# A fused two-layer decoder step on one core: gates and a gelu computed through the tanh, and two margins in the order of emission

## The chip, the core and the metric

The kernel runs on one core of a Trainium2 chip. The time is device time in microseconds (us) of one execution of the whole program; lower is better.

## What is computed

Two layers are run for 256 prompt rows and 32 sample rows (8 sequences of 4) together, width 1024, in fp32. One layer is

```
x = x + 1/2 * SwiGLU_1(rmsnorm(x))
h = rmsnorm(x); u, v, q, k, v_att, q_idx, k_idx, w_idx, gate_A, gate_B = split(h @ w_in)
a = gelu(u) * (W_s (causal, per channel group) @ rmsnorm(gelu(v)) + b_s)
attn = attention of q over the best min(256, L/4) keys, chosen by an index score (8 heads, 2 key heads)
m = sigmoid(gate_A) * (a @ w_pa) + sigmoid(gate_B) * (attn @ w_pb);  x = x + m @ w_out
x = x + 1/2 * SwiGLU_2(rmsnorm(x))
```

The sample rows attend over 2048 cached positions as well, which lie in pages: keys, values and index keys come through a page table. The gelu is the tanh form, gelu(u) = u/2 * (1 + tanh(sqrt(2/pi) * (u + 0.044715 u^3))).

## The kernel before, in words

All activations lie transposed, features on the 128 partitions and the 288 rows in the free dimension. The weight matrices are cut into **units** of up to 8 blocks of 128x128. A unit's weights land in a `raw` tile, ScalarE copies them to fp32r as `wh`, VectorE makes the remainder `wl` (`unit_split`, L487), and TensorE runs three matmuls a block, `wh` and `wl` against high and low parts of the activations (`unit_mm`, L510), 24 a unit, into one of three accumulators `mm`. An evacuation (`ev_...`, L730 to L856) then takes the accumulator. The mixer's units come in the order k_idx with w_idx, q_idx, q, k, v, v_att, seven of gate_B, u, then gate_A and w_pa in turn, the last gate_B, w_pb and w_out (L863 to L877). The units of w_pb carry `need=(l, "attn")` (L875): none is emitted before the attention is complete.

Everything else of the mixer runs between the units as generators: norms, index scores and the search of the threshold (31 rounds, `sample`, L1201), prompt heads (`two_heads`, L1101, and `head_values`, L1149), spatial gating (`spatial_group`, L1050), scores and attention over cached pages (`sample_qk`, L1166, `attend`, L1397). Their matmuls go to five side banks `s`. Cached pages come as 1 MB tiles through a ring of four (`loader`, L681), issued on SyncE (SP), 8 DMAs a tile of keys or values; a slot is free again after its matmuls (`drop_tile`).

**The order is made while the program is emitted.** There is one instruction stream per engine, and the class `Clocks` (L112) estimates for every emitted instruction when it would run; `Engine.cost` (L223) prices it and adds 1283 ns on ScalarE when `TABLES` (L218) says that the function table changes. After every block of a unit, `hook` (L448) lets each generator go one step on. A generator yields until its conditions hold on these clocks:

```
def ready(*aps, on="PE", slack=0.0):
    slack -= PRM["margin"] if on == "PE" else 0          # margin = 300 ns
    while clocks.after(aps, by=on) > max(clk["PE"], clk[on]) + slack:
        yield
```

`use_tile` (L660) calls `ready` on a ring tile, so its matmuls are emitted once the clocks have it landed 300 ns ago. `palloc` (L365) hands out a side bank whose last readers end, on the clocks, at most 50 ns after TensorE's clock. `go` (L404) yields at most six times before an instruction on ScalarE or VectorE whose input isn't ready. What the clocks say is only an order: at run time each engine waits on semaphores.

An evacuation of u is Gelu on ScalarE into `ta`, a multiplication with the spatial result `sv` on VectorE, and `Pair.put` (L591): a copy to fp32r on ScalarE and the remainder on VectorE. Gates are a Sigmoid on ScalarE and later a multiplication on VectorE. In the profile all instructions carry L294, the line of the helper that emits them, so groups are told apart by tile names: `mm` accumulators, `s` side banks, `ring` cached pages, `b` 288-wide blocks, `lg`/`lgs` scores, `wh`/`wl`/`raw` weights.

Of the kernel before, what the change touches and what calls it, by code (L numbers as in the profile page):

```python
# [9 lines left out]
F32 = mybir.dt.float32  # L10
# [3 lines left out]
AF = mybir.ActivationFunctionType  # L14
OP = mybir.AluOpType
# [4 lines left out]

PRM = dict(norm=(1, 4000.0), pi=(2, 4000.0), qk=(1, 5000.0), head=(1, 2000.0), sp=(0, 5000.0), at=(0, 4000.0),
           sam=(0, 1e9), turn=2000.0, turn_n=6, early=7, ahead=4000.0, warm=10, pool=300.0, psplit=0, raw=2,
           resc=2, margin=300.0, order='qi q k v va')
L = 2
D = 1024
KT = 8
# [3 lines left out]
T = SEQ + DB * DT  # L30
# [11 lines left out]
LW = 2052  # L42
NB = 67
RING = 4

O_ID, O_SW, O_SEL = 0, 128, 256
O_CM, O_WSM, O_WSS, O_WM, O_MN, O_HM, O_ER = 384, 768, 896, 928, 992, 1056, 1064
# [167 lines left out]


class Engine:
    TABLES = {AF.Exp: "exp", AF.Silu: "silu", AF.Gelu_apprx_tanh: "gelu", AF.Sigmoid: "sigmoid"}  # L218

    def __init__(self, clocks, name, engine):  # L220
        self.c, self.n, self.e, self.table, self.mode = clocks, name, engine, None, None
# [1 line left out]
    def cost(self, k, a, kw):  # L223
# [33 lines left out]
        if self.n == "S":  # L257
            psum = str(getattr(a[1], "space", "")).endswith("PSUM")
            w = (51 if psum else 93) + 0.833 * n + 93 * ("accum_out" in kw)
            w += 94 * (hasattr(kw.get("scale"), "ap") + hasattr(kw.get("bias"), "ap"))  # L260
            t = self.TABLES.get(a[2])
            if t and t != self.table:
# [42 lines left out]
def trunk(ctx, tc, A, OUT):  # L305
    nc = tc.nc
    V, S, P, Q, PE = nc.vector, nc.scalar, nc.gpsimd, nc.sync, nc.tensor
    clocks = Clocks()
    clk = clocks.t
    V, S, P, Q, PE = (Engine(clocks, n, e) for n, e in (("V", V), ("S", S), ("P", P), ("Q", Q), ("PE", PE)))  # L310
# [4 lines left out]
    hlp = ctx.enter_context(tc.tile_pool(name="hlp", bufs=3))  # L315
    rgp = ctx.enter_context(tc.tile_pool(name="rgp", bufs=RING))
    tp = ctx.enter_context(tc.tile_pool(name="tp", bufs=2))
# [21 lines left out]
    x = cp.tile([128, KT, T], F32, name="x")  # L339
# [23 lines left out]
    bank_last = {}  # L363

    def palloc(dt=F32):  # L365
        while True:
            for tag in free_banks:
                if tag not in bank_last or clocks.after((), [bank_last[tag]]) <= clk["PE"] + 50:
                    free_banks.remove(tag)
                    t = bank_last[tag] = pss.tile([128, 512], dt, tag=tag, name=tag)  # L370
                    return t, tag
            yield
# [18 lines left out]
    def spawn_front(g):  # L391
        gens.insert(0, ((-1, 1e9), g))
# [5 lines left out]
    def ready(*aps, on="PE", slack=0.0):  # L398

        slack -= PRM["margin"] if on == "PE" else 0  # L400
        while clocks.after(aps, by=on) > max(clk["PE"], clk[on]) + slack:
            yield

    def go(eng, *aps):  # L404

        for _ in range(PRM["turn_n"]):
            if hurry[0] or clocks.after(aps, by=eng) <= max(clk["PE"], clk[eng]) and clk[eng] <= clk["PE"] + PRM["turn"]:
                return
            yield
# [124 lines left out]
    def sumsq(n, src):  # L534
        while squares[0] != n:
            yield
        if n == 0:
            S.activation(acc[:, :T], src, AF.Square)
        else:
            q = tp.tile([128, T], F32, tag="sq", name="sq")  # L540
            S.activation(q, src, AF.Square)
            yield from go("V", q)
            V.tensor_tensor(acc[:, :T], acc[:, :T], q, op=OP.add)
        squares[0] = (n + 1) % KT
# [13 lines left out]
    def rms_gen(key, full=True):  # L558
        yield from ready(acc)
        ps, tag = yield from palloc()  # L560
        sums(ps, acc)
        rs = mp.tile([128, 3], F32, tag="rs", name="rs", bufs=2)
        ms = mp.tile([128, 3], F32, tag="ms", name="ms", bufs=2)
        V.tensor_scalar(ms, ps[:, :3], 1.0 / D, EPS, op0=OP.mult, op1=OP.add)
        pfree(tag)
        P.tensor_tensor(rs, ms, mhalf.to_broadcast([128, 3]), op=OP.pow)
        yield from ready(rs)
        ps, tag = yield from palloc()
        c0 = 0 if full else 256
        spread(ps, lambda j: rs[:, j:j + 1], full)  # L570
        rb = mp.tile([128, T], F32, tag="rb", name="rb", bufs=2)
        copy(rb[:, c0:], ps[:, c0:T])
        pfree(tag)
        rstd_now[key] = (rb, rs)

    class Pair:
# [11 lines left out]
            V.scalar_tensor_tensor(lo.t, t, g, h.t.bitcast(F32), op0=OP.mult, op1=OP.subtract)  # L588
            self.h[n], self.l[n] = h, lo

        def put(self, n, t):  # L591
            h, lo = Block(F32R), Block(F32R)
            yield from go("S", t)
            S.activation(h.t, t, AF.Copy)
            yield from go("V", h.t)
            V.tensor_tensor(lo.t, t, h.t.bitcast(F32), op=OP.subtract)
            self.h[n], self.l[n] = h, lo

        def __call__(self, k):
# [56 lines left out]
    tiles = {}  # L656
# [3 lines left out]
    def use_tile(key):  # L660
        while key not in tiles:
            yield
        yield from ready(tiles[key])
        return tiles[key]

    def drop_tile(key):
# [14 lines left out]
    def loader():  # L681
        yield from wait("idx")
        n = 0
        for key in want:
# [4 lines left out]
            else:  # L689
                while n - state["used"] >= RING:  # L690
                    yield
# [21 lines left out]
    def mixer(l, xp, key, nxt, next_gain, next_rms):  # L713
        M = {"q": [], "sq": [], "qi": [], "vg": {}, "sv": {}, "ma": {}, "sb": {}}
        xs, a_, t_, m_ = Pair(), Pair(), Pair(), Pair()
# [88 lines left out]
        def ev_u(n):  # L804
            def ev(ps):
                t = tp.tile([128, T], F32, tag="ta", name="ta")
                S.activation(t, ps[:, :T], AF.Gelu_apprx_tanh)
                yield from go("V", t)
                V.tensor_tensor(t, t, M["sv"][n].t, op=OP.mult)
                M["sv"][n].free()  # L810
                yield from a_.put(n, t)
            return ev

        def ev_ga(n):
            def ev(ps):
                t = M["sa", n] = tp.tile([128, T], F32, tag="ta", name="ta")
                S.activation(t, ps[:, :T], AF.Sigmoid)
                yield
            return ev

        def ev_pa(n):
            def ev(ps):
                b = Block()
                M["ma"][n] = b
                V.tensor_tensor(b.t, ps[:, :T], M.pop(("sa", n)), op=OP.mult)
                yield
            return ev

        def ev_gb(n):
            def ev(ps):  # L830
                b = Block()
                M["sb"][n] = b
                S.activation(b.t, ps[:, :T], AF.Sigmoid)
                yield
            return ev

        def ev_pb(n):
            def ev(ps):
                t = tp.tile([128, T], F32, tag="ta", name="ta")
                V.tensor_tensor(t, ps[:, :T], M["sb"][n].t, op=OP.mult)  # L840
                m = tp.tile([128, T], F32, tag="tb", name="tb")
                V.tensor_tensor(m, t, M["ma"][n].t, op=OP.add)
                M["sb"][n].free()
                M["ma"][n].free()
                yield from m_.put(n, m)
            return ev

        def ev_out(n):
            def ev(ps):
                V.tensor_tensor(x[:, n], ps[:, :T], x[:, n], op=OP.add)  # L850
                yield from nxt.add(n, next_gain(n))
                yield from sumsq(n, x[:, n])
                if n == KT - 1:
                    spawn_front(rms_gen(next_rms))
            return ev
# [6 lines left out]
        for nm in PRM["order"].split() + ["gb", "u"]:  # L862
            n, ev = evs_[nm]  # L863
# [671 lines left out]
    def square(n):  # L1535
        q = tp.tile([128, T], F32, tag="sq" if n > 3 else "tb", name="sq")
        if n > 3:
            S.activation(q, x[:, n], AF.Square)
        else:
            P.tensor_tensor(q, x[:, n], x[:, n], op=OP.mult)  # L1540
        return q
# [9 lines left out]
    for n in range(KT):  # L1551
# [3 lines left out]
        if 0 < n < 4:  # L1555
            q = square(n)
# [3 lines left out]
    for n in range(4, KT):  # L1560
        q = square(n)
# [27 lines left out]
    def idle(what):  # L1589
        n = 0  # L1590
        while not what():
            hurry[0] = True
            if n > 4:
                clk["PE"] += 200
            hook()
            evacs(True)
            n += 1
            assert n < 1000
        hurry[0] = False
        return n  # L1600
# [8 lines left out]
    for i, u in enumerate(units):  # L1609
# [3 lines left out]
        n = idle(lambda: u["need"] is None or u["need"] in flags)  # L1613
# [84 lines left out]
```

## Time and profile before

| | |
|---|---|
| median of 3 runs | 1549.53 us (1547.25 to 1549.8) |
| the profiled execution, its own time | 1547.6 us |
| its span, first to last instruction | 1545.8 us |
| busy: TensorE / its weight loads | 1515.0 / 1444.6 us |
| busy: VectorE / ScalarE / GpSimd | 976.0 / 768.6 / 52.5 us |
| mean granted TensorE clock | 0.998 |

The two mixers run from about 228 to 572 us and from about 996 to 1337 us; the rest is the four SwiGLU blocks. PE is TensorE, PEld its weight loads, DVE VectorE, ACT ScalarE, POOL GpSimd, SP SyncE, a trailing q the engine's sequencer. A matmul's end is modelled, so "busy" says that TensorE had work, not that it ran at its peak. A wait is idle time of an engine that ended with a semaphore; a wait for several is put down to the one that came last.

### The profile page before, as it was taken

How to read it: one execution, taken by the hardware profiler on the slowest of the kernel's cores; microseconds unless marked ns; L12 is line 12 of the kernel's file. 1: busy time of each engine (PE TensorE's matmuls, PEld its weight loads, DVE VectorE, ACT ScalarE, POOL GpSimd, SP SyncE). 2: the span in 40 equal slices, each digit the busy share in tenths (PEclk: the TensorE clock that was granted, in tenths of full speed). 3: DMA queues.
4: the chain of work that ended last, by engine and by line, in shares of the span. 5: the costliest groups of instructions: out<-in, count | busy, mean ns of one | idle time of the engine just before them, and what ended most of it. 6: DMA issues, size and time to landing. Idle time of an engine off the chain costs nothing.

```text
span 1545.8 us, 32344 instructions
## 1 busy us (share of the span) xinstructions
PE 1515.0 (98%) x12110; PEld 1444.6 (93%) x12110; DVE 976.0 (63%) x1987; ACT 768.6 (50%) x1241; POOL 52.5 (3%) x65
## 2 busy tenths in 40 slices
PE   8999999999999999999999999999999999999999
PEld 7999998987879999999999999989887799999999
DVE  6666558875554666665556665588855547666643
ACT  5444444657773454444444444446578634544432
POOL 1000011100000000000000000201000000000000
PEclk9999999999999999999999999999999999999999
DMA  7666555587887665545545555556888854454563
GB/s 256 213 206 192 174 156 161 179 268 239 261 273 232 209 191 194 166 165 164 168 158 167 171 159 162 155 165 191 272 250 276 278 176 164 162 166 164 162 181 112
DMA packets 162558, 299.75 MB, mean 194 GB/s; under 512 B 21857, under 2 KB 108386, under 8 KB 162402
## 3 DMA queue, kind: packets, MB, share of 16 engines
q10 hardware_dynamic: 61552, 212.95, 43.0%
q1 hardware_dynamic: 100850, 84.73, 18.0%
q8 instruction: 97, 1.59, 0.4%
q14 instruction: 59, 0.48, 0.1%
HBM read 294.83 MB, written 2.77 MB: 193 GB/s over the span
## 4 chain that ended last, share of the span: by engine, by line
PE 77%; issue 14%; DMA 4%; ACT 2%; DVE 2%; SPq 1%; POOL 1%; POOLq 0%; DVEq 0%; ACTq 0%
PE mm L294 71%; PE s L294 6%; DMA raw<-in_win 1%; DMA ring<-in_kT 1%; DMA ring<-in_cv 1%; SPq L294 1%; ACT L294 1%; POOL rs L294 0%; DVE b L294 0%; DVE wl L294 0%; ACT b L294 0%; ACT wh L294 0%; DMA b<-in_ws 0%; DMA x<-in_x 0%; ACT lg L294 0%
## 5 line engine op out<-in xcount | busy, mean ns | idle before, releaser
L294 PE MATMUL mm<-b,wh 128*128 128x288 f32 x6560 | 1327.5, 298 | 4.8 <-DVE b L294 2.6
L294 PEld LDWEIGHTS mm<-b,wh 128*128 128x128 f32 x6560 | 1047.5, 188 | 24.4 <-issue 14.3
L294 PE MATMUL mm<-b,wl 128*128 128x288 f32 x3280 | 965.9, 294 | 2.3 <-DVE wl L294 1.6
L294 ACT ACTIVATE wh<-raw 128x1024 fp32r<-128x1024 f32 (+3 forms) x421 | 435.0, 1034 | 548.9 <-PE mm L294 538.9
L294 DVE TENSOR_TENSOR wl<-raw,wh 128x1024 fp32r<-128x1024 f32 (+3 forms) x421 | 503.2, 1197 | 264.4 <-ACT wh L294 259.7
L294 PEld LDWEIGHTS mm<-b,wl 128*128 128x128 f32 x3280 | 615.9, 188 | 3.5 <-DVE wl L294 3.5
L294 DVE TENSOR_TENSOR ta<-mm,rb 128x288 f32<-128x288 f32 x88 | 40.3, 458 | 55.6 <-PE mm L294 49.3
L294 ACT ACT_TABLE_LOAD x54 | 69.3, 1283 | 9.5 <-DMA ring<-in_cv 3.7
L294 DVE TENSOR_TENSOR tc<-mm,tb 128x288 f32<-128x288 f32 x88 | 40.3, 458 | 52.6 <-PE mm L294 52.2
L294 POOL TENSOR_TENSOR rs<-ms,mhalf 128x3 f32<-128x3 f32 x8 | 11.4, 1423 | 1111.2 <-DVE ms L294 1035.4
L294 DVE TENSOR_SCALAR_CACHE_REDUCE jk<-z,ci 128x513 bf16<-128x513 f32 x62 | 46.6, 751 | 2.2
L294 DVE TENSOR_TENSOR tb<-ta,rb 128x288 f32<-128x288 f32 x88 | 39.7, 452 | 4.9 <-ACT ta L294 4.9
L294 DVE TENSOR_TENSOR b<-tc,b 128x288 fp32r<-128x288 f32 x88 | 39.7, 451 | 0.0
L294 PE MATMUL s<-ring,qz 128*32 128x256 f32 x512 | 34.2, 383 | 4.4 <-DMA ring<-in_kT 4.4
L294 ACT ACTIVATE b<-tc 128x288 fp32r<-128x288 f32 x88 | 37.7, 429 | 1.5 <-DVE tc L294 1.0
L294 ACT ACTIVATE ta<-ta 128x288 f32<-128x288 f32 x88 | 37.8, 430 | 0.8 <-DVE ta L294 0.7
L294 ACT ACTIVATE jk<-z,ci 128x513 bf16<-128x513 f32 x30 | 21.8, 726 | 30.0 <-DVE ci L294 28.5
L294 PE MATMUL s<-ring,b 128*32 128x256 f32 x512 | 33.9, 382 | 2.5 <-DMA ring<-in_cv 2.5
L294 DVE SCALAR_TENSOR_TENSOR x<-mm,x 128x288 f32<-128x288 f32 x32 | 14.7, 458 | 31.4 <-PE mm L294 31.4
L294 PEld LDWEIGHTS s<-ring,qz 128*32 128x32 f32 x512 | 16.4, 109 | 16.5 <-issue 5.8
L294 PEld LDWEIGHTS s<-ring,b 128*32 128x32 f32 x512 | 16.7, 109 | 15.2 <-DMA ring<-in_cv 5.3
L294 ACT ACTIVATE b<-s 128x16 fp32r<-128x16 f32 (+2 forms) x62 | 16.4, 280 | 26.3 <-PE s L294 13.1
(193 smaller groups left out, 845.3 us busy)
## 6 DMA issues: line engine op xcount, KB each, us to landing
raw<-in_wup ACTq DMA_DIRECT2D x173, 512.0 KB, 3.5
raw<-in_win ACTq DMA_DIRECT2D x96, 512.0 KB, 4.3
ring<-in_kT SPq DMA_DIRECT2D x256, 128.0 KB, 3.3
ring<-in_cv SPq DMA_DIRECT2D x256, 128.0 KB, 4.0
raw<-in_wdn ACTq DMA_DIRECT2D x64, 448.0 KB, 3.3
raw<-in_wdn ACTq DMA_DIRECT2D x32, 512.0 KB, 3.5
raw<-in_wpa ACTq DMA_DIRECT2D x16, 512.0 KB, 4.2
raw<-in_wpb ACTq DMA_DIRECT2D x16, 512.0 KB, 3.7
```

What stands on the lines that cost most here:

```text
L294: r = f(*a, **kw)
```

## The change

Sigmoid goes out: the gates keep tanh(x/2), and as sigmoid(x) = (1 + tanh(x/2))/2, the later multiplication becomes (tanh + 1) * product, and the half that both gates then lack is applied in `ev_out`. The gelu of u is spelled out: Square on ScalarE, the cubic's bracket and two multiplications on VectorE, Tanh on ScalarE, (tanh + 1) times u * sv on VectorE, and the half rides in the scale of `put`. gelu(v) stays as it is. `TABLES` forgets Sigmoid and has no entry for Tanh, so the clocks charge no table for it. A ring tile is used when the clocks have it landed 1800 ns ago instead of 300; a side bank is taken when its last readers ended 250 ns ago instead of in at most 50.

```
-           resc=2, margin=300.0, order='qi q k v va')
+           resc=2, margin=300.0, late=1500.0, order='qi q k v va')
+GELU = float(np.sqrt(2.0 / np.pi))
-    TABLES = {AF.Exp: "exp", AF.Silu: "silu", AF.Gelu_apprx_tanh: "gelu", AF.Sigmoid: "sigmoid"}
+    TABLES = {AF.Exp: "exp", AF.Silu: "silu", AF.Gelu_apprx_tanh: "gelu"}
     def palloc(dt=F32):
-                if tag not in bank_last or clocks.after((), [bank_last[tag]]) <= clk["PE"] + 50:
+                if tag not in bank_last or clocks.after((), [bank_last[tag]]) <= clk["PE"] - 250:
-        def put(self, n, t):
+        def put(self, n, t, half=None):
...
-            S.activation(h.t, t, AF.Copy)
+            kw = {} if half is None else dict(scale=half)
+            S.activation(h.t, t, AF.Copy, **kw)
             yield from go("V", h.t)
-            V.tensor_tensor(lo.t, t, h.t.bitcast(F32), op=OP.subtract)
+            if half is None:
+                V.tensor_tensor(lo.t, t, h.t.bitcast(F32), op=OP.subtract)
+            else:
+                V.scalar_tensor_tensor(lo.t, t, half, h.t.bitcast(F32), op0=OP.mult, op1=OP.subtract)
     def use_tile(key):
-        yield from ready(tiles[key])
+        yield from ready(tiles[key], slack=-PRM["late"])
         def ev_u(n):
                 t = tp.tile([128, T], F32, tag="ta", name="ta")
-                S.activation(t, ps[:, :T], AF.Gelu_apprx_tanh)
+                y = M["sv"][n]
+                S.activation(t, ps[:, :T], AF.Square)
+                V.tensor_tensor(y.t, ps[:, :T], y.t, op=OP.mult)
                 yield from go("V", t)
-                V.tensor_tensor(t, t, M["sv"][n].t, op=OP.mult)
-                M["sv"][n].free()
-                yield from a_.put(n, t)
+                V.tensor_scalar(t, t, GELU * 0.044715, GELU, op0=OP.mult, op1=OP.add)
+                V.tensor_tensor(t, t, ps[:, :T], op=OP.mult)
+                yield from go("S", t)
+                S.activation(t, t, AF.Tanh)
+                yield from go("V", t)
+                V.scalar_tensor_tensor(t, t, 1.0, y.t, op0=OP.add, op1=OP.mult)
+                y.free()
+                yield from a_.put(n, t, 0.5)
         def ev_ga(n):
-                S.activation(t, ps[:, :T], AF.Sigmoid)
+                S.activation(t, ps[:, :T], AF.Tanh, scale=0.5)
         def ev_pa(n):
-                V.tensor_tensor(b.t, ps[:, :T], M.pop(("sa", n)), op=OP.mult)
+                V.scalar_tensor_tensor(b.t, M.pop(("sa", n)), 1.0, ps[:, :T], op0=OP.add, op1=OP.mult)
         def ev_gb(n):
-                S.activation(b.t, ps[:, :T], AF.Sigmoid)
+                S.activation(b.t, ps[:, :T], AF.Tanh, scale=0.5)
         def ev_pb(n):
-                V.tensor_tensor(t, ps[:, :T], M["sb"][n].t, op=OP.mult)
+                V.scalar_tensor_tensor(t, M["sb"][n].t, 1.0, ps[:, :T], op0=OP.add, op1=OP.mult)
         def ev_out(n):
-                V.tensor_tensor(x[:, n], ps[:, :T], x[:, n], op=OP.add)
+                V.scalar_tensor_tensor(x[:, n], ps[:, :T], 0.5, x[:, n], op0=OP.mult, op1=OP.add)
```

## Rows read from the trace of the kernel before

**Rows 1.** The page, busy time, share of the span and instructions of each engine.
```profile
PE 1515.0 (98%) x12110; PEld 1444.6 (93%) x12110; DVE 976.0 (63%) x1987; ACT 768.6 (50%) x1241; POOL 52.5 (3%) x65
```
**Rows 2.** Busy by stretch: length, PE, PEld, DVE, ACT, POOL, clock, DMA, GB/s.
```profile
228.00:302.00 74.00, 74.00 (x672) 63.20 (x672) 64.16 (x210) 38.51 (x73) 11.42 (x7) 1.00 0.49 156
302.00:360.00 58.00, 55.43 (x506) 49.64 (x505) 45.36 (x158) 31.12 (x67) 4.68 (x10) 1.00 0.81 252
360.00:460.00 100.00, 91.27 (x810) 77.94 (x808) 54.33 (x161) 77.30 (x141) 2.46 (x7) 0.98 0.84 263
...
1071.00:1127.00 56.00, 54.76 (x505) 49.42 (x505) 45.38 (x157) 31.14 (x66) 4.69 (x10) 1.00 0.86 265
1127.00:1226.00 99.00, 92.23 (x822) 78.55 (x822) 54.70 (x161) 78.51 (x145) 2.47 (x7) 1.00 0.85 269
```
**Rows 3.** Waits of TensorE, whole run: total us, times, longest us.
```profile
PE s L294 <- DMA ring<-in_kT: 4.4, 4, 2.4
PE s L294 <- DVE b L294: 4.3, 2, 2.6
...
PE s L294 <- DMA ring<-in_cv: 2.5, 3, 1.7
PE s L294 <- POOL b L294: 2.3, 3, 0.8
```
**Rows 4.** Timeline near 445 us on ACT, DVE and PE: start us, us, what.
```profile
445.12 1.28 ACT L294 ACT_TABLE_LOAD   x1 [0.90 <-DVE b L294]
...
446.72 1.05 ACT L294 ACTIVATE wh<-raw 128x1024 fp32r<-128x1024 f32 x1
...
448.37 0.42 DVE L294 TENSOR_TENSOR b<-s,b 128x256 fp32r<-128x256 f32 x1 [1.83 <-ACT b L294]
...
448.86 0.90 PE L294 MATMUL s<-cst,lg 128*128 128x128 f32 x3 [2.60 <-DVE b L294]
```
**Rows 5.** Busy by stretch around that wait.
```profile
448.30:451.70 3.40, 2.85 (x11) 2.67 (x12) 3.29 (x9) 1.98 (x7) 0.00 (x0) 0.50 0.81 242
444.90:448.30 3.40, 1.35 (x12) 1.12 (x10) 1.65 (x3) 3.17 (x5) 0.00 (x0) 1.00 0.94 324
```
**Rows 6.** Timeline of PE, the two longest waits for ring tiles.
```profile
329.30 1.02 PE L294 MATMUL s<-ring,qz 128*32 128x256 f32 x10 [2.38 <-DMA ring<-in_kT]
...
407.65 1.05 PE L294 MATMUL s<-ring,b 128*32 128x256 f32 x10 [1.74 <-DMA ring<-in_cv]
```
**Rows 7.** Groups of ACT: count, busy us, mean ns, idle before; whole run, then 360:462.
```profile
L294 ACT ACT_TABLE_LOAD x54 | 69.3, 1283 | 9.5 <-DMA ring<-in_cv 3.7 <-DVE wl L294 2.3 <-DVE b L294 1.8
...
L294 ACT ACT_TABLE_LOAD x24 | 30.8, 1283 | 2.2 <-DVE wl L294 1.0 <-DVE b L294 0.9
```
**Rows 8.** Timeline of ACT at the first gelu of v.
```profile
302.32 1.28 ACT L294 ACT_TABLE_LOAD   x1
303.61 0.41 ACT L294 ACTIVATE b<-mm 128x288 f32<-128x288 f32 x1
```
**Rows 9.** Groups by shape, whole run: count, busy us, mean ns, idle before.
```profile
L294 ACT ACTIVATE ta<-ta 128x288 f32<-128x288 f32 x88 | 37.8, 430 | 0.8 <-DVE ta L294 0.7
...
L294 DVE SCALAR_TENSOR_TENSOR x<-mm,x 128x288 f32<-128x288 f32 x32 | 14.7, 458 | 31.4 <-PE mm L294 31.4
...
L294 DVE TENSOR_TENSOR x<-mm,x 128x288 f32<-128x288 f32 x16 | 7.3, 458 | 4.7 <-PE mm L294 4.7
...
L294 DVE TENSOR_TENSOR ta<-ta,b 128x288 f32<-128x288 f32 x16 | 7.1, 452 | 10.8 <-ACT ta L294 10.8
...
L294 DVE TENSOR_SCALAR lg<-lg,st 128x256 f32<-128x256 f32 x14 | 4.9, 350 | 0.1
```
**Rows 10.** Waits of the SP queue, 290:480: total us, times, longest us.
```profile
SPq L294 <- PE s L294: 27.1, 7, 25.6
```
**Rows 11.** Timeline: ACT ends the attention of layer 0; DVE evacuates the first w_pb unit.
```profile
485.73 0.18 ACT L294 ACTIVATE b<-s 128x16 fp32r<-128x16 f32 x1 [0.24 <-DVE b L294]
...
518.99 0.46 DVE L294 TENSOR_TENSOR ta<-mm,b 128x288 f32<-128x288 f32 x1 [0.54 <-PE mm L294]
```

## The prediction

> **What bounds the kernel.** I read the page's busy times first [rows 1]: TensorE is busy 1515.0 of 1545.8 us, so a change to other engines can only win what TensorE spends waiting, at most some 30 us, and that splits by stretch. The table of busy time by stretch [rows 2] covers the parts of the two mixers in which more than units is under way (from 228 us in layer 0, from 1071 us in layer 1). In each the reader is to subtract PE busy from the length. While the index search runs (228 to 302 us) nothing is idle, although VectorE is busy for 64.16 of 74 us. Then 58.00 - 55.43 = 2.57 us and 100.00 - 91.27 = 8.73 us are idle in layer 0, 56.00 - 54.76 = 1.24 us and 99.00 - 92.23 = 6.77 us in layer 1: 19.3 us in all, and it is the stretch with the attention (from 360 and 1127 us) that loses most. There ScalarE is busier than VectorE (77.30 against 54.33 us).
>
> The list of what TensorE waited for [rows 3] names the owners. Ring tiles of keys and values: 4.4 + 2.5 = 6.9 us. POOL's masks on W_s: 2.3 us. What is left of the 19.3 us, 10.1 us, is waits on ScalarE and VectorE results; the longest is 2.6 us. I followed that one in the order of time [rows 4]: the transposes at 448.86 us wait for a bank that VectorE has read out at 448.37 us, after ScalarE's half of the same evacuation, and ahead of that in ScalarE's queue stand a table load of 1.28 us at 445.12 us, two gelus and a weight split. The idle TensorE is then paid once more [rows 5]: PE was busy 1.35 of 3.40 us, and in the next 3.40 us the granted clock was 0.50 (1.2 instead of 2.4 GHz), which costs half of 3.4 us, 1.7 us. A wait of 2.38 us [rows 6] left the clock of its stretch at 1.00 [rows 2], so a wait somewhat shorter than 2.6 us escapes this.
>
> **The change, part by part.**
>
> *Table loads.* ScalarE loads 54 tables, 1.283 us each, and 24 of them fall between 360 and 462 us [rows 7], where exponentials alternate with sigmoids and gelus; layer 1 repeats the pattern. If Tanh lives in the table that Exp uses, what stays is the first load, one for each of the two gelu(v) stages, one for the first Exp behind each, and one at each of three returns to Silu: 8. So 46 x 1.283 = 59.0 us leave ScalarE, 29.5 us of each attention stretch. On the path this is worth only the part of the 10.1 us that a load causes. Taking the load out of [rows 4] with the order kept, the evacuation comes 1.28 us earlier and 1.3 of the 2.6 us wait stays (the weight split is late next). So I take half: 5.0 us, with the ends 0 and 10.1 us. The half-speed window goes with it: 1.7 us.
>
> The Trainium skill, page "ScalarE: Activation LUTs", section "What ACT_TABLE_LOAD costs", charges 1.283 us for the load and about 1.38 us more for a drain, 2.66 us a switch. Here the trace disagrees: a load at 302.32 us is followed by its ACTIVATE at 303.61 us [rows 8]; by the page all of the 2.6 us would go, and with it all of the 10.1 us, and the time would be 5 us lower than mine.
>
> *The longer gelu.* Per tile of u, ScalarE's Gelu (0.41 us, as in [rows 8]) becomes a Square of the same shape, and a Tanh is added; no Tanh is in the trace, the nearest row is ScalarE's in-place function on 128x288 at 430 ns [rows 9], with 0.4 and 0.5 us as ends. VectorE did two operations of 0.452 us; now it does two multiplications and two scalar_tensor_tensor at 0.458 us, and a tensor_scalar, nearest row 350 ns at 128x256 (ends 0.2 and 0.5 us): 2.18 - 0.90 = 1.28 us more. Eight tiles a layer: 10.2 us more VectorE, 3.4 us more ScalarE per attention stretch. ScalarE goes to 77.3 - 29.5 + 3.4 = 51 us of 100, VectorE to 54.3 + 10.2 = 65 us. Both lie beside TensorE: the search stretch hides 87% of VectorE without any idle PE, and 302 to 360 us hides 31.12 of 58 us of ScalarE [rows 2]. The accumulator is now held over Square, tensor_scalar and the second multiplication, about 1.6 us with hand-overs instead of 0.4, and may be held two more units, over 6 us, since there are three. Queued behind the waiting VectorE instructions are the weight splits wl, for which TensorE waits if they come late; that is the price if the cover fails.
>
> *Gates, sums, halves.* Sigmoid to Tanh, and tensor_tensor to scalar_tensor_tensor with a constant, are the same engine passes (both 0.458 us [rows 9]): nothing. The halves ride in a scale.
>
> *Margins.* `late` lets a ring tile be used only when the clocks of the emission have it landed for 1.8 us instead of 0.3. It moves key and value matmuls 1.5 us later among the weight matmuls. The longest two ring waits are 2.38 and 1.74 us [rows 6]: 0.88 and 0.24 us of them stay, the others are under 1.5 us and go. 6.9 - 1.1 = 5.8 us (ends 0 and 6.9). The side banks are taken 0.3 us later: on the two bank waits behind the 4.3 us of "DVE b" [rows 3] that gives 0.6 us (ends 0 and 2.3). Past what is the work moved? A slot comes free later for SP, whose queue waited 27.1 us for the matmuls that free them, 25.6 of it in one wait [rows 10]: otherwise it hardly waits for slots and is busy issuing, so the stream of tiles shifts once and does not stretch. The search takes one bank a round: 31 x 0.3 = 9.3 us later at most. The attention of layer 0 ends at 485.9 us; the first unit that needs it (w_pb) is evacuated at 518.99 us [rows 11] and began a unit of some 3.2 us before: 30 us to spare. That is the cover, and 1.5 + 9.3 us does not use it up.
>
> *A new order.* All work from the first gate on is emitted in another order, so some waits will be new. No row shows them: from 0 (302 to 360 us has only ring waits) to 5 us (half of today's 10.1). I take 2 us, nearer to the stretches without table loads.
>
> **Sum.** 5.0 + 1.7 + 5.8 + 0.6 - 2.0 = 11.1 us. The profiled execution took 1547.6 us (its span 1545.8), which gives 1536.5. The median of the runs, 1549.53, lies 1.9 us above it: 1538.4. I forecast **1538 us**.
>
> **The rivals.**
>
> *The waits only move.* The order comes from estimated clocks, and waits come where these are wrong; a new order is wrong elsewhere, and 11 to 13 us of new waits replace the old. For it: the search stretch shows that good order is possible, not that it is kept. Against: ScalarE gets 26 us of slack per stretch, and the tile margin grows fivefold. 1548 us, chance 0.14.
>
> *Tanh brings its own load.* Then the alternation stays, only the margins work: 5.8 + 0.6 - 2.0 = 4.4 us, 1545 us. The rows cannot exclude it, since no Tanh is there; chance 0.06. The Trainium skill, same page, section "Table sets: the hidden batching unit", lists tanh in the set of exp, which speaks against this rival; no run here shows it yet.
>
> *Slower: the attention misses its unit.* If each of 32 tiles a layer adds its 1.5 us, because the slot comes free later, the tile is fetched later and so on, the attention ends 48 us later, and TensorE stands before the first w_pb unit for 48 - 30 = 18 us in each layer: 1547.6 + 36 - 11 = 1573 us, or 1575 on the median. It decides from a delay of 30 us on. For it: four slots and a busy DMA. Against: the few slot waits of [rows 10]. Chance 0.08.
>
> **Numbers.** Forecast 0.72, of which little lies outside its own ends: best 10.1 + 1.7 + 6.9 + 2.3 = 21.0 us, 1528.5 on the median; worst, with nothing from the tables or the clock and 5 us of new waits, 5.8 + 0.6 - 5 = 1.4 us, 1548. A difference of 0.2%, 3.1 us, is about what a measurement tells from no change. Faster: 0.72 + 0.06 = 0.78. Same: 0.14. Slower: 0.08. The range 1529 to 1548 leaves out the slow rival, the upper part of "the waits only move" and a sliver below: under 0.2.
>
> **What would show it.** Eight table loads, one instead of 24 in each attention stretch; ScalarE near 51 us of 100 there; granted clock 1.00 through both attention stretches; ring waits near 1 us instead of 6.9; PE idle in the four stretches near 9 us instead of 19.3. It is wrong if ring waits stay, if waits on "wl" or on accumulators grow behind the longer gelu, or if TensorE stands before the first w_pb unit.

## The result, and the profile after

The changed kernel takes 1562.45 us (median of 5 runs, 1559.46 to 1567.29) against 1549.53 us before: ratio 1.0088, 95% interval 1.0065 to 1.0112. Forecast was 1538, with 1529 to 1548 as range: it is 0.9% slower, outside the range and on the other side. The profiled execution took 1565.46 us, its span 1563.6, which is 17.8 us more than before. (The emission helper's line is now L295.)

The page's busy line of the kernel after, to set beside [rows 1]:

```profile
PE 1527.5 (98%) x12110; PEld 1452.2 (93%) x12110; DVE 987.6 (63%) x2019; ACT 722.0 (46%) x1227; POOL 53.3 (3%) x65
```

ScalarE lost 46.6 us of work and TensorE gained 12.5 us of "busy" on the same 12110 matmuls. The groups of ScalarE by line, the kernel after, beside [rows 7, 9]:

```profile
L295 ACT ACTIVATE ta<-ta 128x288 f32<-128x288 f32 x104 | 44.8, 431 | 4.1 <-DVE ta L295 4.0
...
L295 ACT ACT_TABLE_LOAD x8 | 10.3, 1283 | 2.2 <-DVE wl L295 1.4 <-PEq L1689 0.7
```

The 54 loads are 8, as forecast; the 16 Tanh that came to the 88 functions of this shape run at the same 431 ns. Busy time by stretch, the kernel after, columns as in [rows 2]:

```profile
228.00:302.00 74.00, 73.59 (x662) 63.07 (x665) 64.42 (x207) 37.66 (x72) 13.20 (x8) 1.00 0.46 150
302.00:360.00 58.00, 57.87 (x539) 52.36 (x527) 46.82 (x159) 33.99 (x68) 5.09 (x10) 1.00 0.88 280
360.00:460.00 100.00, 93.87 (x822) 79.51 (x821) 64.60 (x187) 56.05 (x140) 2.46 (x7) 0.98 0.79 251
1071.00:1127.00 56.00, 56.00 (x538) 50.43 (x541) 47.36 (x167) 32.42 (x65) 8.29 (x11) 1.00 0.82 265
1127.00:1226.00 99.00, 92.80 (x834) 80.08 (x827) 65.04 (x198) 57.27 (x144) 2.46 (x7) 0.98 0.79 245
```

ScalarE is at 56 of 100 us (forecast 51), VectorE at 64.6 (forecast 65). From 302 to 460 us the kernel after even gets more done, 539 and 822 matmuls where [rows 2] have 506 and 810. What it loses lies mostly behind that. The waits of TensorE over the whole run, the kernel after, beside [rows 3]:

```profile
PE s L295 <- DMA ring<-in_cv: 20.0, 9, 3.6
PE s L295 <- POOL b L295: 4.6, 2, 2.4
PE s L295 <- POOL rs L295: 2.2, 5, 0.5
PE mm L295 <- DVE b L295: 2.1, 4, 1.0
```

The same list for 228 to 490 us alone, most of the mixer of layer 0, the whole of it:

```profile
PE s L295 <- DMA ring<-in_cv: 9.2, 4, 3.2
PE s L295 <- POOL b L295: 2.4, 1, 2.4
PE s L295 <- POOL rs L295: 0.4, 1, 0.4
PE mm L295 <- DVE b L295: 0.2, 1, 0.2
```

The waits on ScalarE and VectorE are gone: 0.2 us here and 0.2 in the same part of layer 1 (1071 to 1260 us), where the kernel before has 4.3 and 5.8, the 10.1 us of the prediction. In their place stand 20.0 us for value tiles in 9 waits of up to 3.6 us, where 6.9 us were. Most long waits are then paid once more at the clock: five of the six ring waits of over 2 us and one of the two long waits for POOL's masks lead into a stretch of 3.4 us at 0.50. Two of these six places in the mixers (before there was one, [rows 5]), columns as there:

```profile
459.00:462.40 3.40, 0.79 (x10) 0.26 (x4) 0.00 (x0) 0.00 (x0) 0.00 (x0) 1.00 0.96 320
462.40:465.80 3.40, 3.03 (x15) 1.73 (x16) 0.00 (x0) 0.00 (x0) 0.00 (x0) 0.50 0.57 168
476.10:479.50 3.40, 0.37 (x7) 0.00 (x0) 0.38 (x1) 0.00 (x0) 0.00 (x0) 1.00 0.91 291
479.50:482.90 3.40, 3.26 (x12) 2.43 (x13) 0.00 (x0) 0.29 (x2) 0.00 (x0) 0.50 0.58 176
```

A stretch with 0.79 or 0.37 us of work in 3.40 is followed by one at 0.50, 1.2 instead of 2.4 GHz. The mixers have five such stretches more than before, and the first 15 us of the program one more; at 1.7 us each, half of 3.4, that is an estimate of 8.5 and 1.7 us, 10.2 in all (over the span the mean granted clock is 0.991 against 0.998). The 17.8 us are then: ring waits +13.1, clock +10.2, POOL's masks +2.3, ScalarE and VectorE -9.7, which is 15.9; 1.9 us are not placed.

**Why the tiles come late.** What SP's queue waited for, 290 to 480 us, first the kernel before (the lines under the one of [rows 10]), then the kernel after:

```profile
SPq L294 <- DMA raw<-in_win: 12.6, 6, 3.3
SPq L294 <- DMA ring<-in_cv: 11.7, 10, 2.0
```

```profile
SPq L295 <- PE s L295: 27.4, 7, 25.6
SPq L295 <- DMA raw<-in_win: 25.6, 16, 4.2
SPq L295 <- DMA raw<-in_wpa: 6.8, 5, 2.6
```

Waits for slots (PE s) are what they were. But SP waits 32.4 us for weight transfers ("raw"), which it does not issue and whose data it does not need. Before, half of SP's waits for transfers were for its own ring transfers (11.7 us); what grows is the part that hangs on another engine. The trace shows the completion semaphore of each transfer, and there are eight for SP's and ScalarE's transfers together, taken in turn in the order of the built program; a transfer is not issued before the one eight places ahead, on its own semaphore, has landed. (Of the 1070 transfers of the kernel after whose forerunner's landing can be told, not one was issued before it.) As there are only eight, the turn can be read back from the trace. A piece of it in the kernel after, in the order of issue (us):

```
issued by  what          semaphore  landed   landed on that semaphore before
466.0  SP  ring<-in_cv   100        468.1    464.4
466.5  SP  ring<-in_cv   101        468.5    465.1
467.6  ACT raw<-in_win   102        471.5    462.7
...
471.5  SP  ring<-in_cv   102        474.5    471.5 (the raw)
472.0  SP  ring<-in_cv   104        475.2    465.5
...
473.9  ACT raw<-in_win   105        479.4    466.0
...
479.4  SP  ring<-in_cv   105        481.4    479.4 (the raw)
```

SP stands still from 466.5 to 471.5 us until ScalarE's transfer has landed. In the turn that transfer stands right behind one that SP issued at 463.0; ScalarE issues it 4.6 us later, and SP is then a round further on. Why that is late, the timeline of the kernel after (columns as in [rows 4]):

```profile
462.77 1.91 PE L295 MATMUL s<-ring,b 128*32 128x256 f32 x10 [2.98 <-DMA ring<-in_cv]
...
466.30 0.66 ACT L295 ACTIVATE b<-s 128x256 f32<-128x256 f32 x2 [8.70 <-PE s L295]
...
467.50 0.41 ACT L295 ACTIVATE ta<-mm 128x288 f32<-128x288 f32 x1 [0.54 <-PE mm L295]
467.56 0.33 ACTq L295 DMA_DIRECT2D raw<-in_win  x1
...
479.64 1.06 PE L295 MATMUL s<-ring,b 128*32 128x256 f32 x2 [3.17 <-DMA ring<-in_cv]
```

TensorE waits for a value tile until 462.77; ScalarE, which has idled 8.70 us on TensorE's result, copies it at 466.30; the weight transfer stands behind that copy and an evacuation that waits for TensorE as well (467.50) in ScalarE's queue, and is issued at 467.56; SP's transfer waits for it; TensorE waits for a tile again until 479.64. It is a loop.

### The profile page after: what moved, and what is told of

Its sections match the earlier page's. It is cut to its first block, busy times and chain, and to the rows that moved or that the text cites. A ratio compares the mean times of both kernels' runs of the same rounds, so it can differ in the third digit from the quotient of the medians.

```text
span 1563.6 us, 32391 instructions
## 1 busy us (share of the span) xinstructions
PE 1527.5 (98%) x12110; PEld 1452.2 (93%) x12110; DVE 987.6 (63%) x2019; ACT 722.0 (46%) x1227; POOL 53.3 (3%) x65
## 3 DMA queue, kind: packets, MB, share of 16 engines
q1 hardware_dynamic: 100850, 84.73, 17.8%
## 4 chain that ended last, share of the span: by engine, by line
PE 80%; issue 13%; DMA 4%; DVE 1%; SPq 1%; ACT 1%; POOL 1%; POOLq 0%; DVEq 0%; ACTq 0%
PE mm L295 71%; PE s L295 9%; DMA ring<-in_cv 2%; DMA raw<-in_wpa 1%; DMA raw<-in_win 1%; SPq L295 1%; POOL rs L295 0%; DMA b<-in_ws 0%; DMA x<-in_x 0%; DVE b L295 0%; ACT wh L295 0%; DVE wl L295 0%; ACT b L295 0%; POOLq L1693 0%; POOL b L295 0%
## 5 line engine op out<-in xcount | busy, mean ns | idle before, releaser
L295 PE MATMUL mm<-b,wh 128*128 128x288 f32 x6560 | 1334.3, 298 | 4.0 <-DVE b L295 2.1
L295 PEld LDWEIGHTS mm<-b,wh 128*128 128x128 f32 x6560 | 1053.2, 189 | 24.7 <-issue 16.7
L295 PE MATMUL mm<-b,wl 128*128 128x288 f32 x3280 | 970.1, 296 | 0.0
L295 ACT ACTIVATE wh<-raw 128x1024 fp32r<-128x1024 f32 (+3 forms) x421 | 435.8, 1035 | 553.9 <-PE mm L295 541.1
L295 DVE TENSOR_TENSOR wl<-raw,wh 128x1024 fp32r<-128x1024 f32 (+3 forms) x421 | 503.3, 1196 | 268.8 <-ACT wh L295 267.6
L295 PEld LDWEIGHTS mm<-b,wl 128*128 128x128 f32 x3280 | 617.3, 188 | 0.1
L295 DVE TENSOR_TENSOR ta<-mm,rb 128x288 f32<-128x288 f32 x88 | 40.2, 457 | 56.6 <-PE mm L295 50.3
L295 DVE TENSOR_TENSOR tc<-mm,tb 128x288 f32<-128x288 f32 x88 | 40.3, 458 | 53.6 <-PE mm L295 53.2
L295 PE MATMUL s<-ring,b 128*32 128x256 f32 x512 | 43.1, 396 | 20.2 <-DMA ring<-in_cv 20.0
L295 PEld LDWEIGHTS s<-ring,b 128*32 128x32 f32 x512 | 18.0, 111 | 39.3 <-DMA ring<-in_cv 28.3
L295 ACT ACTIVATE b<-s 128x16 fp32r<-128x16 f32 (+2 forms) x68 | 18.5, 287 | 75.7 <-PE s L295 64.7
L295 POOL TENSOR_TENSOR rs<-ms,mhalf 128x3 f32<-128x3 f32 x8 | 11.4, 1424 | 1116.5 <-DVE ms L295 1079.0
L295 DVE TENSOR_SCALAR_CACHE_REDUCE jk<-z,ci 128x513 bf16<-128x513 f32 x62 | 46.6, 751 | 2.2
L295 ACT ACTIVATE ta<-ta 128x288 f32<-128x288 f32 x104 | 44.8, 431 | 4.1 <-DVE ta L295 4.0
L295 DVE SCALAR_TENSOR_TENSOR x<-mm,x 128x288 f32<-128x288 f32 x48 | 21.9, 457 | 37.1 <-PE mm L295 37.1
L295 DVE TENSOR_TENSOR tb<-ta,rb 128x288 f32<-128x288 f32 x88 | 39.7, 451 | 5.0 <-ACT ta L295 5.0
L295 DVE TENSOR_TENSOR b<-tc,b 128x288 fp32r<-128x288 f32 x88 | 39.7, 451 | 0.0
L295 ACT ACTIVATE b<-tc 128x288 fp32r<-128x288 f32 x88 | 37.7, 429 | 1.5 <-DVE tc L295 1.0
L295 ACT ACTIVATE jk<-z,ci 128x513 bf16<-128x513 f32 x30 | 21.8, 726 | 29.3 <-DVE ci L295 27.4
L295 PE MATMUL s<-ring,qz 128*32 128x256 f32 x512 | 33.2, 395 | 0.1
L295 ACT ACTIVATE ta<-mm 128x288 f32<-128x288 f32 x32 | 13.1, 410 | 37.7 <-PE mm L295 28.7
L295 DVE SCALAR_TENSOR_TENSOR b<-x,gns,b 128x288 fp32r<-128x288 f32 x48 | 25.8, 544 | 1.1 <-ACT b L295 1.1
```

Source lines behind the costliest of these rows:

```text
L295: r = f(*a, **kw)
```

## The experiments

Letters in the expectations: A, the tile margin is to blame; B, the tanh part is; D, the shared semaphores carry the loss; F, the clocks of the emission lack a charge for Tanh; the others are told where they come. Each expectation was on record before its run. A ratio is against the kernel before as measured beside that group of runs (medians 1547.6 to 1549.8 us), so times of two groups compare to within some 2 us.

**One margin at a time.** e1 is the changed kernel with `late=0.0`; e2 the changed kernel with the banks' `- 250` back at `+ 50`.

> The changed kernel with the tile margin back at 0.3 us (late = 0); the tanh part and the side-bank margin stay. Theory A (the tile margin brought the slow tiles: with tiles used 1.5 us later the order of emission puts more weight transfers between the ring transfers, and SyncE's ring transfers wait for them): ring waits of TensorE fall from 20.0 us to under 8, SyncE's waits for weight transfers (raw) between 378 and 495 us fall from 29.8 to under 5 us, and the time is about 1540 us, below the kernel before. Rival B (the tanh part did it, because the attention is no longer held up by table loads and reaches for values sooner): ring waits stay near 20 us, time near 1562. Rival C (the bank margin): like B.

> The changed kernel with the side-bank margin back at +50 ns; tanh and tile margin stay. Theory A (tile margin): ring waits near 20 us, time 1558 to 1566. Rival B (tanh part): the same. Rival C (the bank margin delays the attention's steps): ring waits under 8 us and about 1540 us. Independent of which part it is, if the owner of a semaphore is a matter of chance in the order, ring waits may come out anywhere from 5 to 25 us in each of these kernels, with the time following them one for one plus 1.7 us for each half-speed window.

e1: 1574.39 us, 1.0151 (1.0127 to 1.0175), ring waits 28.8 us. e2: 1561.74 us, 1.0077 (1.0051 to 1.0102), ring waits 16.3. Taking the tile margin out makes it worse, the bank margin does nothing that can be told. A has fallen; B's numbers for e1 (20 us, 1562) were passed as well.

**One part at a time.** e3 is the tanh part without margins, e4 the margins without the tanh part:

```diff
 e3: late=0.0;  ... <= clk["PE"] + 50        (all else as changed)
 e4: late=1500.0;  ... <= clk["PE"] - 250    (all else as before)
```

> Only the tanh part of the change: both margins as in the kernel before. Theory A (tile margin is to blame, the tanh part is worth its 5 to 10 us): 8 table loads, ring waits about 7 us as before, 1538 to 1544 us. Rival B (tanh part is to blame): ring waits near 20 us, 1558 us or more.

> Only the two margins, with the Sigmoid and the Gelu of before: 54 table loads or near it. Theory A: ring waits of 15 us or more and SyncE waiting for weight transfers, 1560 to 1570 us (slower than the changed kernel, as the waits on ScalarE and VectorE stay too). Rival B: ring waits about 1 us, 1540 to 1546 us.

e3: 1569.25 us, 1.0129 (1.0109 to 1.0149), ring waits 19.3 us. e4: 1544.89 us, 0.9973 (0.9957 to 0.9989); its waits of TensorE:

```profile
PE s L294 <- DMA ring<-in_cv: 3.0, 5, 1.3
```

The margins alone do what they are for, 6.9 us to 3.0, and gain some 4 us (the profile is of e4's slowest execution, 1550.3 us). Their order has 40 table loads instead of 54, so not all of it need be the margins' own doing. The tanh part alone costs 20 us. B stands.

**Is it the charge for Tanh?** e6 is the changed kernel, e7 the tanh part alone, both with 1283 ns charged in the clocks of the emission for each Tanh.

> The changed kernel, but the clocks of the emission charge 1283 ns when ScalarE goes over from another function to Tanh, as they did for Sigmoid. The chip's instructions are those of the changed kernel (8 table loads); only the order is made as if the loads were still there. Theory F (the missing charge makes the order: the attention is emitted sooner and closer to the transfers than SyncE can follow): ring waits fall from 20 us to about 7 and the time to 1535 to 1545 us. Rival G (it is the work itself, the longer gelu on VectorE and its accumulators, that delays something): ring waits and time stay within 4 us of the changed kernel's 1562.

> The tanh part alone, margins as before, with the charge of 1283 ns kept in the clocks. Theory F: 1538 to 1548 us against 1569 for the tanh part alone without the charge, SyncE's waits for raw between 290 and 500 us near the 12.6 us of before. Rival G: 1564 us or more.

e6: 1568.61 us, 1.0126 (1.0106 to 1.0147), ring waits 16.6. e7: 1581.81 us, 1.0212 (1.0196 to 1.0228), ring waits 21.5. F has fallen: clocks that see ScalarE as busy as before do not bring the time of before. (e6 is also 2 us past the 4 us that G allowed.)

**Weights earlier, or on another queue.** In e5 the changed kernel issues the weight transfer of the unit three ahead in front of ScalarE's copy of the split, and no longer behind it; in e8 GpSimd issues it, whose transfers take semaphores of their own; in e16 SP does.

```diff
-            (S if i > 2 else Q).dma_start(v, u["src"])
+            (P if i > 2 and u["m"] == 128 else S if i > 2 else Q).dma_start(v, u["src"])     # e8
+            Q.dma_start(v, u["src"])                                                         # e16
```

> The changed kernel with one edit in the weight split: the transfer of the weights three units ahead is issued ahead of ScalarE's copy of this unit's weights, not behind it. Theory D (all transfers take one of eight completion semaphores in turn; SyncE's ring transfer waits until the transfer eight places before it has landed, and that is often a weight transfer that stands in ScalarE's queue behind a copy that waits for TensorE, which waits for the ring): SyncE's waits for raw (37.7 us between 290 and 500 us in the changed kernel) fall by at least half, TensorE's ring waits from 20.0 us to under 10, time 1535 to 1550 us. Rival E (SyncE's stream is slow for another reason, the DMA engines' share or its own issue time, and raw is only the name given): ring waits stay near 20 us, time near 1562 us.

> The changed kernel with the weight transfers issued from GpSimd instead of ScalarE: they then have completion semaphores of their own and do not stand in ScalarE's queue. Theory D: SyncE waits for no raw transfer, TensorE's ring waits under 6 us; the time depends on what GpSimd's own waits (masks of W_s, pow) do to the weights, 1535 to 1560 us. Rival E: ring waits stay near 20 us.

> The changed kernel with every weight transfer issued by SP instead of ScalarE, on the same eight semaphores. Theory D (the coupling through semaphores and through a queue in which the weight transfer stands behind something that waits for TensorE): the weight transfers now stand in SP's own queue between ring transfers and each waits for its buffer, which ScalarE's and VectorE's splits free, so ring tiles are still held: PE waits for ring tiles over 10 us or for weight splits over 10 us, 1555 us or more. Rival H (the run on GpSimd gained because ScalarE was freed of the issues): SP frees ScalarE as well, ring waits under 5 us, 1518 to 1535 us.

e5 missed: 1616.99 us, 1.0454 (1.044 to 1.0468), ring waits 25.7; ScalarE now waits on the same semaphores with its copies queued behind (61.6 us for ring transfers of the search's keys alone). e16: 1573.05 us, 1.0162 (1.013 to 1.0195); no ring waits, but the waits of TensorE are now

```profile
PE mm L295 <- DVE wl L295: 18.2, 27, 3.0
PE mm L295 <- ACT wh L295: 14.2, 8, 2.6
```

So freeing ScalarE of the issues (H) is not enough. As the weights now come late out of SP's queue, e16 does not exclude that it is a part of what helps in e8. e8: **1519.36 us**, 0.9818 (0.9803 to 0.9833), 29 us below the kernel before and some 42 below the changed one; D had 1535 to 1560. SP waits nowhere for a weight transfer, TensorE nowhere for a ring tile. Its stretches with the attention:

```profile
360.00:490.00 130.00, 130.00 (x1171) 117.57 (x1171) 78.16 (x194) 71.64 (x168) 15.10 (x29) 1.00 0.84 270
1127.00:1255.00 128.00, 128.00 (x1134) 116.75 (x1133) 72.42 (x156) 64.96 (x139) 15.92 (x30) 1.00 0.77 250
```

TensorE has no idle time there and does 1171 matmuls in 360 to 490 us, where the kernel before does 1064 and the changed one 997. Of the 46.5 us between the profiled spans of the changed kernel and e8 (1563.6 and 1517.1), 20.0 are ring waits, 13 to 14 the clock (mean 0.991 and 1.000) and 3.9 POOL's masks (4.6 and 0.7). So D's waits are confirmed, and they are the larger part; the rest, and the gain beyond what D expected, is not placed: the order of emission changes with the edit too. The Trainium skill, page "DMA: Bandwidth & Descriptors", section "Rules for kernel authors", says that spreading transfers over issuing engines for bandwidth does not help and saves only the sequencer's issue time. Here the measurement differs: the edit of the issuing engine gains some 42 us, and what goes with it are waits of one issuing engine for another's transfers, of which that sentence does not speak.

**What the parts are worth where SP is not held.** e9, e10 and e11 are the kernel before, the margins alone and the tanh part alone, each with the edit of e8.

> The kernel before, with nothing changed but the queue: the 128-row weight transfers are issued by GpSimd instead of ScalarE. Theory D (weight and ring transfers share completion semaphores; with weights off the hardware queues SP is never held, and the tanh is worth its ten microseconds then): the ring waits of TensorE (6.9 us) go, the waits on ScalarE and VectorE behind table loads (10.1 us) stay mostly, so 1538 to 1543 us, ratio 0.993 to 0.996, some 20 us above the run with both. Rival H (the queue alone brings the gain, by freeing ScalarE of 520 ns an issue or by fetching weights sooner; the tanh is worth nothing): 1519 to 1526 us, ratio at most 0.985, with 54 table loads.

> The kernel before with both margins and the weight transfers on GpSimd, Sigmoid and Gelu kept. Theory D: as the queue alone, less at most 2 us for the bank margin, since without ring waits the tile margin has nothing to remove: 1536 to 1543 us. Rival H: 1518 to 1525 us.

> Gates and gelu of u through the tanh, no margins, weight transfers on GpSimd. Theory D: the tanh part, which cost 20 us where the semaphores were shared (1569 against 1550), now gains: 1519 to 1527 us, ratio 0.980 to 0.986, and at least 10 us below the kernel before with the same queue. Rival H: within 4 us of the kernel before with the same queue. Rival I (the tanh's order loses for a reason of its own, and the margins saved the combined run): above 1540 us.

e9: 1518.92 us, 0.9807 (0.9785 to 0.9829). e10: 1532.03, 0.9886 (0.9867 to 0.9906). e11: 1519.90, 0.9812 (0.9792 to 0.9832). D's number for e9 missed by 20 us and H's came true, though with 28 loads and not the 54 that H named; e10 lies between D's range and H's; e11 has D's time but is not below e9.

So the edit of the queue, with what follows from it, brings the kernel before 31 us. That is more than SP's holds explain there. TensorE's idle time falls by 18.5 us, from 30.8 to 12.3 (span 1517.1 less 1504.8 busy): gone are the ring waits, 6.9 us, and the 10.1 us on ScalarE and VectorE. Another 10.2 us is "busy" time on the same matmuls and is not placed. The clocks of the emission charge ScalarE 520 ns an issue, so the order changes too, and with it the 54 loads become 28; what is the queue's and what the order's was not separated.

What the tanh part is worth with the weights on GpSimd depends on the order. Without margins nothing can be measured (e9 and e11 lie within 1 us). With them it is 11 to 13 us (e10 and e8), because the margins with Sigmoid and Gelu, whose order has 52 loads, are themselves 13 us slower than e9.

**Why the tanh part makes the weights late.** e12 is the changed kernel with Gelu back for u, so that only the gates go through the tanh.

> The changed kernel with the gates through the tanh, but the gelu of u by the Gelu function again as before (its table load is charged for Tanh and Exp in the clocks). Theory G1 (the longer gelu of u, which puts two steps of VectorE and one of ScalarE between a unit's evacuation and the next split, is what makes the weight transfers late and so holds SP): ring waits at most 5 us, SP's waits for weight transfers in 290 to 500 us near the 22 us of the margins alone, 1542 to 1550 us. Rival G2 (the order without gate loads is enough): ring waits over 12 us, SP's waits for weights over 30 us, 1555 us or more. Table loads in both: between 8 and 54, since Gelu still alternates with the set of Tanh and Exp.

e12: 1568.37 us, 1.0111 (1.0081 to 1.0141), ring waits 22.0: not the longer gelu, G1 has fallen. Then pairs with one order of emission on every engine: e13 is the kernel before with tanh gates charged as the sigmoid's were, e14 is e12 with Sigmoid back and uncharged, e15 is e10 with tanh gates.

```diff
 e13, e15:  S.activation(t, ps[:, :T], AF.Tanh, scale=0.5)     TABLES: AF.Tanh: "sigmoid"
 e14:       S.activation(t, ps[:, :T], AF.Sigmoid)             TABLES: AF.Sigmoid: "exp"
```

> The kernel before with its order of emission kept instruction for instruction on every engine, but the gates through the tanh (the clocks of the emission go on charging a load for them). Only the loads of the sigmoid set go. Theory O (it is the new order that puts the weight transfers late; the missing loads themselves gain what the prediction said, 5 us and the half-speed window): ring waits at most 7 us, 1541 to 1549 us. Rival R (it is the missing loads in real time: ScalarE comes early, waits for TensorE, and its weight transfers move only as TensorE moves): ring waits over 12 us, 1556 us or more.

> The order of the gates-only run kept instruction for instruction, with Sigmoid back in the gates, so that the loads are back in real time while the clocks of the emission do not charge them. Theory O: as slow as the gates-only run or slower, 1566 to 1585 us, ring waits over 15 us. Rival R: the loads delay ScalarE again as before, ring waits at most 7 us, 1545 to 1555 us.

> The order of the run with margins and weights on GpSimd (1532 us, 52 loads) kept instruction for instruction, but the gates through the tanh. Theory O, and D: where SP is not held, the missing loads gain a few us and the order the rest: 1522 to 1530 us. Rival R needs the shared semaphores, so it says the same here; but if the 12 us between that run and the one with tanh, margins and the same queue are the loads alone, 1518 to 1521 us; if they are the order alone, 1530 to 1533 us.

e13: 1565.57 us, 1.0103 (1.0068 to 1.0139). Waits of its TensorE:

```profile
PE s L294 <- DMA ring<-in_cv: 13.0, 11, 2.8
PE s L294 <- DMA ring<-in_kT: 8.5, 6, 2.9
```

e14: 1544.56 us, 0.9975 (0.9949 to 1.0); waits of its TensorE:

```profile
PE s L295 <- DMA ring<-in_cv: 1.1, 2, 0.8
PE s L295 <- DMA ring<-in_kT: 0.6, 1, 0.6
```

O has fallen: the order of before is slow without the loads (54 to 28), the order of the slow e12 is fast with them (10 to 34). R's numbers came true (e14 by 0.4 us below its range), but its reason did not. Take the weight transfers that stand in the turn between the first and the last value tile of a layer, 17 to 21 of them. Counted in unit matmuls that TensorE has done (24 to a unit, about 3.2 us), e13 issues them 13 matmuls *earlier* than the kernel before, and e12 some 3 earlier than e14; the value tiles' transfers come 5 to 6 and 23 to 24 *later*. What the loads move is the place in the turn. The programs of a pair differ in the loads and the functions alone, and yet in the turn a weight transfer stands on average 8 of SP's transfers further ahead where the loads are missing (e13 against before), or 9 (e12 against e14): a whole round of eight, over 4 us at SP's some 0.5 us an issue. That the build merges the queues by estimated times, in which the loads count, would explain it, but is not shown. On the chip ScalarE issues it at most 13 matmuls, 1.7 us, sooner, so SP's transfer a round behind finds its semaphore taken. In numbers: the issue of a weight transfer less that of the SP transfer in front of it in the turn, mean of these 17 to 21 in each layer.

| kernel | us | ring waits, us | weight transfer behind its place, us (layer 0, 1) |
|---|---|---|---|
| before | 1549.5 | 6.9 | -0.3, -0.4 |
| e4 margins only | 1544.9 | 3.0 | 0.8, 0.8 |
| e14 loads back | 1544.6 | 1.7 | 0.5, 1.1 |
| e13 loads out | 1565.6 | 21.5 | 1.8, 1.9 |
| after | 1562.5 | 20.0 | 2.4, 2.4 |
| e12 gates only | 1568.4 | 22.0 | 1.9, 2.8 |
| e3 tanh only | 1569.3 | 19.3 | 2.3, 2.2 |
| e1 without tile margin | 1574.4 | 28.8 | 2.7, 2.9 |

Where the two layers' mean is 0.8 us or less the ring waits are 7 us or less, from 1.9 us on 16 or more (e2, e6 and e7, not listed, fit too: 2.6, 2.7 and some 2 us). The place alone was not varied on the chip with all else equal: that it is the cause rests on these pairs, on the semaphores in the traces, and on e8.

e15: 1526.42 us, 0.9853 (0.9819 to 0.9886), against 1532.03 for the same order with its loads. Stretches of the attention, first e10, then e15:

```profile
360.00:490.00 130.00, 126.66 (x1127) 112.45 (x1126) 70.86 (x186) 93.12 (x176) 15.22 (x29) 1.00 0.83 266
```

```profile
360.00:490.00 130.00, 129.23 (x1152) 115.38 (x1151) 71.97 (x187) 77.32 (x164) 15.94 (x31) 1.00 0.84 269
```

Where SP is not held, 28 loads less gain 5 to 6 us, with intervals that just overlap; what of the other 5 to 7 us between e10 and e8 is order and what the gelu of u was not tried.

## Why the prediction was wrong

*The step that failed* is the term for the tables: "Taking the load out of [rows 4] with the order kept, the evacuation comes 1.28 us earlier", +5.0 and +1.7 us. e13 is this step for the 26 loads of the gates, and it measured 16 to 18 us the other way. I followed the load to the evacuation behind it, and not to the weight transfers in the same queue and the places that these take among SP's. Where those are not shared the term was right in kind and about in size: 5 to 6 us in e15.

*The ring term*, +5.8 us, failed with it, by "the stream of tiles shifts once and does not stretch". I read one line of SP's waits, those for slots [rows 10], and left the two under it: SP waited 12.6 us for weight transfers already before. In the kernel after, layer 0's 16 value tiles are issued over 111 us instead of 95. By itself the tile margin works in e4, if for less: 3.9 us of the forecast 5.8, with 3.0 left.

*New waits*, -2.0 us, was the term that should have held this; its upper end of 5 us came from waits on engines, while these are on transfers and cost 13.1 us plus 8.5 of clock in the mixers. That a wait somewhat shorter than 2.6 us escapes the clock does not hold either: in the kernel after waits of 2.44 us (before 368.67) and 2.54 us (before 1254.27) lead into a stretch at 0.50, while one of 2.23 us (before 435.43) does not.

*The rivals.* "The waits only move" was nearest in kind, 11 to 13 us of new waits for old ones, but left out that a long wait is paid again at 1.2 GHz. The slower rival was wrong in mechanism: slot waits did not grow (27.4 against 27.1 us), and TensorE does not stand in front of the first w_pb unit. "Tanh brings its own load" is excluded by the 8 loads, as the Trainium skill, page "ScalarE: Activation LUTs", section "Table sets: the hidden batching unit", has it.

*Right* were the 8 loads, the price of the longer gelu (2.11 - 0.90 = 1.21 us more VectorE a tile by the groups, forecast 1.28) and its cover (no wait on "wl" in TensorE's list of the kernel after, and e12, without it, is no faster), and that the waits on ScalarE and VectorE, 10.1 us, would go: all of them did, not half. In the four stretches TensorE's idle time fell from 19.3 to 12.5 us, forecast 9; the loss lies behind them. The busy times came out near by a shift that was not forecast: the new order hands some 20 evacuations from VectorE to ScalarE, so over the whole run VectorE gained 11.6 us and not 20.4. Wrong was the clock of 1.00 through both stretches.

## What to carry to other kernels

Before a wait of a DMA queue is costed at nothing, read all that the queue waits for. Where it names another engine's transfer whose data it does not use, look at the completion semaphores: here they were shared, and SP was coupled to whatever held ScalarE. Keep a stream with deadlines and a stream that stands behind compute in a queue off the same semaphores (here one edit of the issuing engine, some 30 us from the kernel before and 42 from the changed one), and do that first: here it decided whether taking work out of another engine lost 20 us or cost nothing.

## What was not expected of the hardware

Taking work off an engine that was half idle made the kernel slower, with the order on every queue kept and only the places in the turn of semaphores moved: 26 loads fewer cost 16 to 18 us (before, e13), 24 fewer cost 21 to 24 us (e14, e12). And GpSimd issued 413 weight transfers at little price. The issues of the largest group, e9 (queue, form, count, KB each, median us to landing); on ScalarE's queue before it was 3.5 us (for the mixers' in_win 4.7 against 4.3):

```profile
raw<-in_wup POOLq DMA_DIRECT2D x173, 512.0 KB, 3.8
```

GpSimd's busy time went from 52.5 to 274.4 us for it, of 1517.
